# Expert results written to a row per token and choice instead of added to a row per token

## The chip, the cores and the metric

The kernel runs on one core of a Trainium2 chip. The metric is device time in microseconds (us). Engines: PE (TensorE, matrix products), DVE (VectorE), ACT (ScalarE), Pool (GpSimd), and SP, which here does nothing but issue transfers. Sixteen DMA engines carry out the transfers of all queues; SP's queue is q1 in the profile, Pool's queue q0. All data are float32; T = 1024 tokens, D = 1024 features.

## What is computed

Two transformer blocks one after the other: attention, a gated convolution FFN and a per-layer gate; then retention and a gated delta rule, and a mixture of 32 experts, closed by a norm. The change is in the mixture and the norm behind it:

```python
flat_e = (g_idx * EXPERTS_PER_GROUP + e_local).reshape(-1)   # two experts per token
order = jnp.argsort(flat_e)
tok = order // TOP_K
xs = xf[tok]
hid = silu(ragged_dot(xs, w1, group_sizes)) * ragged_dot(xs, w3, group_sizes)
ys = ragged_dot(hid, w2, group_sizes) * gate.reshape(-1)[order][:, None]
ffn = segment_sum(ys, tok, num_segments=n)
...
x = x + gate2[:, None, :] * ffn
return rmsnorm(x, final_norm_w)
```

So each token gets the sum of three rows: its own x (called x4 below) and the results of its two experts.

## The kernel before

The first block fills the span up to about 1430 us, the second block's mixers go to about 2260, then come the second half of the output projection with the router (2260 to 2360), the routing tables (2362 to 2385), the experts (2392 to 3025) and the final norm (3021 to 3061).

**Places.** The experts stand at 32 places of fixed size. The first three take 128 rows each; the others are ordered by their number of tokens, and the size of a place falls from 256 rows (two tiles) to 32 by a fixed list of steps. Places of up to 64 rows from the 16th on are "small". What doesn't fit is left to a loop (`left_over`, L1625 and after), which runs zero times for these inputs. All 36 tiles together have 3008 rows; the routing needs 2048. The order of work mixes large and small places and is written out by hand.

**Tables.** One-hot products give, for each row of each tile, its token plus one (0 where the row is empty). From this DVE makes two index tables: `tokI` for gathers, where an empty row names token 0, and `tabI` for scatters, where an empty row names a row of its own behind the tokens. `eidI` is the table of experts by place that SP reads to address weights. An empty row has gate 0.

**A place.** `gather` (L1467) is an indirect DMA on Pool: rows of h2 in DRAM into `xg`. PE transposes them, ACT and DVE split them in two parts (`xTh`, `xTl`). The twelve 512 KB blocks of an expert's weights come by `fetch` (L1238) on SP into a ring of 28 buffers (`r`, `Bh`, `Bl`, `x`), in order: each waits for its buffer to be free and for the transfer eight before it. Each block is split into `hi` (ACT, or Pool for some blocks, L80 and L86) and `lo` (DVE, L91). Products give `h`, `hid` (DVE, L1522 and L1542) and `y`. ACT copies y (L1580), Pool multiplies by the row `g2_row` (L1581) and issues the scatter (L1582), an indirect DMA that adds the tile's rows to rows of `y_d` in DRAM. `y_d` has T + 128 rows; x4 has been written to its first T rows, and the 128 behind them, cleared from a zeroed tile, take the empty rows. The two last places (30 and 31) scatter nothing: `keep` (L1585) holds their rows in `both`, in two parts.

**Final norm.** Eight fetches bring `y_d` back as tiles R[0] to R[7] (they wait for the last scatter), then the norm's weight row `fn`. `add_rows(t)` multiplies the one-hots of the last places' tokens by `both` on PE (L1683), adds the result to R[t] on DVE (L1684) and squares on ACT (L1685). `scales` (L1689 and the lines of `rsqrt`) makes the scale of four tiles in small DVE operations, `finish` scales a tile by it and by `fn`: odd tiles on ACT and Pool (L1694, L1695), even ones on DVE (L1697). Then the tile goes out (L1698). The order is four additions, scales, four additions, four finishes, scales, four finishes; the scheduler interleaves it on each engine.

**At the start of the FFN** (about 709 us) Pool only clears two columns of a buffer `gpad` (L614) now and then, SP loads weights and the convolution's taps `cw` (L580), and the additions of the convolution (L621) run on DVE.

Of the kernel before, what the change touches and what calls it, by code (L numbers as in the profile page):

```python
# [11 lines left out]
F32 = mybir.dt.float32  # L12
# [9 lines left out]
T = 1024  # L22
D = 1024
# [7 lines left out]
# steps of the delta rule after each product of the token-major projections, and how many of these come before them  # L31
LEAD, PACE = 3, (3,)
# blocks of an expert whose high parts are Pool's
HI_POOL = (2, 5, 8, 11)
# experts fetched before the counts are known; places with two tiles
NS, TWO = 3, 4
# buffers of weights (0 to 7: room of R; 8 to 23: room of B; others: their own) in the order of their use, and how many are filled after each tile
BUFS = [24, 25, 26] + [0, 1, 2, 8, 9, 10, 3, 11, 12, 13, 4, 14, 15, 5] + list(range(16, 24)) + [6, 7, 27, 28]
AHEAD = [1, 2, 2, 4, 4, 3, 1, 0]
# kinds of the places in their order: s fetched early, T two tiles, M up to 128 rows, L up to 64 rows  # L40
ORDER_OF = "sss" + "LLT" * 4 + "MMM" + "ML" * 6 + "LL"
# last steps: add rows, scales, finish a tile; tiles finished on Pool
GROUP = 3
# chunks of the retention that come before the output projection
RET, OUT_LAG, R_LAG = 2, 3, 2
FIN, FIN_POOL = "aaaacaaaaffffcffff", (1, 3, 5, 7)
# rows of a place: (from this place on, how many more)
STEPS = ((0, 128), (NS, 128), (NS + 1, -32), (NS + 2, -32), (NS + TWO, -64), (10, -32), (16, -32), (22, -16), (28, -16))
# first of the small places
# [3 lines left out]
def constants():  # L53
    """Tables that depend on shapes alone, one float32 array of 128 rows."""
# [28 lines left out]
def split(nc, src, hi, lo, hi_engine="act", lo_engine=None):  # L83
    """src = hi + lo exactly; both parts fit the float32r format."""
# [9 lines left out]
def rsqrt(nc, pool, x, y, n, tag="rsq"):  # L94
    """y = x ** -0.5 for small [128, n] tiles (first guess from the bits, then Newton)."""
# [10 lines left out]
def mm3(nc, ps, ah, al, bh, bl, start, stop, **kw):  # L106
    """ps += (ah + al)^T (bh + bl) without the product of the two low parts."""
    nc.tensor.matmul(ps, ah, bh, start=start, stop=False, **kw)  # L108
    nc.tensor.matmul(ps, ah, bl, start=False, stop=False, **kw)  # L109
    nc.tensor.matmul(ps, al, bh, start=False, stop=stop, **kw)  # L110


class Halves:
    """[128, NK, T] kept as two tiles, one for each half of T"""
# [11 lines left out]
def tile_kernel(ctx: ExitStack, tc: tile.TileContext, a: dict, out: bass.AP):  # L126
# [18 lines left out]
    def turn(out_, in_):  # L145
        """out_ <- in_^T"""
# [8 lines left out]
    # ------------------------------------------------------------------ x^T  # L155
# [6 lines left out]
    with ph:  # L162
# [45 lines left out]
        def forget_gates():  # L208
            """c = cumsum(log_sigmoid(f)), kept as -c in two parts"""
# [35 lines left out]
        def project(hp, begin=False):  # L245
            """k, q, v of two heads, feature-major; v is then turned to keys on partitions."""
# [123 lines left out]
        def attend(hp):  # L370
            """Scores of a block of queries go ahead of the products with v of the block before it."""
# [21 lines left out]
        # the first product starts on half of the tokens  # L393
# [13 lines left out]
        # ---- o^T of the other pairs, and p @ ple_w_proj (kept in DRAM), under the last pair  # L407
# [28 lines left out]
    # ------------------------------------------------------- shared from here on  # L436
    TW = dict(reuse_waits="tile")

    def row(pool_, src, name, bufs=None):
        """One row of DRAM on all partitions."""  # L440
# [4 lines left out]
    def layer_norm(pl, rs, g, b):  # L445
        """r <- LN(r) * g + b for a few tiles of tokens."""
# [15 lines left out]
    def rms_scale(pl, rs, y, junk):  # L462
        """y[:, i] <- (mean(rs[i]^2) + 1e-6)^-0.5"""
# [7 lines left out]
    def turn_in(psp, r, t, tag="pt"):  # L471
        """Bh/Bl[:, :, tile t] <- r^T in two parts."""
# [10 lines left out]
    def parts(src, pool_=None):  # L483
        """One [128, 1024] block of weights as two parts."""
# [6 lines left out]
    def load_res(w, more):  # L491
        """[1024, 1024] weights, one pair of parts for each row block."""
        return [parts(w[k * 128:(k + 1) * 128, :], pool_=None if k < 5 else more) for k in range(NK)]

    def token_mm(psp, t, w):
        """tile t of (B^T)^T @ w, 1024 columns in two banks."""
# [10 lines left out]
    # ------------------------------------------- output projection, residual, LN  # L507
# [22 lines left out]
    # ------------------------------------- modulation rows: silu(c) @ w_ada + b_ada  # L530
# [31 lines left out]
    # ------------------------------------------------------------- gated conv FFN  # L562
# [13 lines left out]
    with tc.tile_pool(name="ffn", bufs=2, **TW) as fp:  # L576
        w_up = a["ffn_w_up"][0]
# [10 lines left out]
        def need(key, ahead):  # L588
            """Weights in the order of their use, some ahead of it."""
# [1149 lines left out]
```

## Time and profile before

| | us |
|---|---|
| median of the runs | 3064.95 |
| lowest to highest of the three runs | 3062.79 to 3067.33 |
| span of the profiled execution | 3061.3 |
| PE busy in it | 2866.5 (94%) |
| DVE, ACT, Pool busy | 1765.7, 1016.4, 644.7 |
| moved by DMA | 432.4 MB, 141 GB/s over the span |

The median lies 3.65 us above the profiled span. A window's row gives, for each engine, busy time and the number of instructions, then the clock granted to PE (1.00 is the full 2.4 GHz), the mean busy share of the DMA engines (it can come out a little over 1) and what they moved. In a timeline a row is one instruction or a run of alike ones: start, duration, engine, line, operation, what it writes and reads, and in brackets how long the engine stood idle before it and what ended that.

### The profile page before, as it was taken

What the parts mean: (1) busy time and instruction counts of PE and PEld (TensorE: products, weight loads), DVE (VectorE), ACT (ScalarE), POOL (GpSimd) and SP (SyncE); (2) the same over time, 40 slices, a digit from 0 to 9 for tenths busy, and PEclk for the clock granted to TensorE, in tenths of its full rate; (3) what the DMA queues carried; (4) which work ended last, traced back from release to release, by engine and by line L of the source; (5) the groups of instructions that cost most, each with busy time, mean ns of one, the idle gap of its engine ahead of it and who ended that gap; (6) DMA issues with size and microseconds to landing.
All of it is one profiled execution on the core that took longest, in us unless ns stands there. A gap on an engine that the chain in (4) does not pass through costs nothing. (4 is left out here: it accounts for less than half of the span.)

```text
span 3061.3 us, 38090 instructions
## 1 busy us (share of the span) xinstructions
PE 2866.5 (94%) x13899; PEld 2168.0 (71%) x13899; DVE 1765.7 (58%) x3066; ACT 1016.4 (33%) x1773; POOL 644.7 (21%) x622
## 2 busy tenths in 40 slices
PE   7999999899999999999989999999996799998985
PEld 5777777677787877877767888888775655465441
DVE  4666666556555454555956545544578743358654
ACT  3555555612121221221324321222222433244432
POOL 2333332100000000000120023211222434444542
PEclk9999999999999999999998999999998899999997
DMA  3110111424233232232244412222557799998997
GB/s 99 36 32 29 35 32 41 163 79 111 69 97 97 69 110 72 73 110 83 97 80 89 92 66 66 80 76 76 195 166 248 252 339 334 329 322 290 362 374 279
DMA packets 272681, 432.39 MB, mean 141 GB/s; under 512 B 40550, under 2 KB 135910, under 8 KB 272364
## 3 DMA queue, kind: packets, MB, share of 16 engines
q1 hardware_dynamic: 264908, 405.41, 40.3%
q0 software_dynamic: 7584, 24.52, 3.4%
q8 instruction: 111, 1.82, 0.2%
q14 instruction: 78, 0.64, 0.1%
HBM read 373.61 MB, written 56.25 MB: 140 GB/s over the span
## 5 line engine op out<-in xcount | busy, mean ns | idle before, releaser
L108 PE MATMUL g<-Bh,hi 128*128 128x512 f32 x896 | 357.9, 400 | 5.1 <-ACT hi L86 3.9
L109 PE MATMUL g<-Bl,hi 128*128 128x512 f32 x896 | 356.7, 398 | 3.3 <-DVE Bl L91 3.3
L110 PE MATMUL g<-Bh,lo 128*128 128x512 f32 x896 | 356.9, 398 | 1.1 <-DVE lo L91 1.1
L108 PE MATMUL g<-hi,Bh 128*128 128x512 f32 x704 | 282.8, 406 | 4.9 <-ACT hi L86 4.0
L109 PE MATMUL g<-lo,Bh 128*128 128x512 f32 x704 | 281.7, 402 | 0.7 <-DVE lo L91 0.7
L110 PE MATMUL g<-hi,Bl 128*128 128x512 f32 x704 | 282.2, 402 | 0.0
L86 ACT ACTIVATE hi<-wst 128x1024 fp32r<-128x1024 f32 x122 | 128.3, 1058 | 430.9 <-PE g L110 207.8
L91 DVE TENSOR_TENSOR lo<-wst,hi 128x1024 fp32r<-128x1024 f32 x122 | 149.0, 1226 | 187.4 <-ACT hi L86 186.6
L108 PEld LDWEIGHTS g<-Bh,hi 128*128 128x128 f32 x896 | 169.1, 189 | 47.2 <-ACT hi L86 4.6
L109 PEld LDWEIGHTS g<-Bl,hi 128*128 128x128 f32 x896 | 169.4, 189 | 45.1 <-DVE Bl L91 4.1
L110 PEld LDWEIGHTS g<-Bh,lo 128*128 128x128 f32 x896 | 169.5, 189 | 42.8 <-DVE lo L91 1.9
L614 POOL MEMSET gpad<- 128x2 f32 x22 | 2.2, 100 | 787.6 <-DVE cacc L621 658.2
L108 PE MATMUL g<-Bh,wh 128*128 128x512 f32 x384 | 155.3, 404 | 5.4 <-DVE k L262 3.6
L108 PEld LDWEIGHTS g<-hi,Bh 128*128 128x128 f32 x704 | 133.2, 189 | 33.8 <-ACT hi L86 5.2
L109 PE MATMUL g<-Bl,wh 128*128 128x512 f32 x384 | 155.9, 406 | 0.0
L110 PE MATMUL g<-Bh,wl 128*128 128x512 f32 x384 | 155.3, 404 | 0.0
L109 PEld LDWEIGHTS g<-lo,Bh 128*128 128x128 f32 x704 | 133.6, 190 | 29.3 <-DVE lo L91 1.8
L110 PEld LDWEIGHTS g<-hi,Bl 128*128 128x128 f32 x704 | 133.3, 189 | 29.4 <-DVE Bl L91 0.9
L109 PE MATMUL h<-lo,xTh 128*128 128x512 f32 (+2 forms) x320 | 130.2, 407 | 16.0 <-DVE lo L91 16.0
L331 POOL TENSOR_SCALAR P<-P,l 128x384 f32<-128x384 f32 (+7 forms) x128 | 96.6, 759 | 224.3 <-DVE l L330 162.0
L109 PE MATMUL g<-lo,hh 128*128 128x512 f32 x352 | 140.3, 399 | 0.0
L108 PE MATMUL g<-hi,hh 128*128 128x512 f32 x352 | 139.9, 397 | 0.0
(525 smaller groups left out, 6333.6 us busy)
## 6 DMA issues: line engine op xcount, KB each, us to landing
r<-in_w_dram SPq DMA_DIRECT2D x107, 512.0 KB, 10.7
Bh<-in_w_dram SPq DMA_DIRECT2D x105, 512.0 KB, 10.5
Bl<-in_w_dram SPq DMA_DIRECT2D x104, 512.0 KB, 10.7
x<-in_w_dram SPq DMA_DIRECT2D x68, 512.0 KB, 10.5
wst<-in_w_ada_dram SPq DMA_DIRECT2D x48, 512.0 KB, 3.9
wst<-in_ffn_w_up_dram SPq DMA_DIRECT2D x44, 512.0 KB, 3.7
wst<-in_w_in_dram SPq DMA_DIRECT2D x32, 512.0 KB, 6.0
wst<-in_attn_w_in_dram SPq DMA_DIRECT2D x24, 512.0 KB, 3.8
```

Of the source, the lines that this page charges most:

```text
L86: nc.scalar.activation(hi, src, AF.Copy)
L91: (lo_engine or nc.vector).tensor_tensor(lo, src, hi, op=OP.subtract)
L108: nc.tensor.matmul(ps, ah, bh, start=start, stop=False, **kw)
L109: nc.tensor.matmul(ps, ah, bl, start=False, stop=False, **kw)
L110: nc.tensor.matmul(ps, al, bh, start=False, stop=stop, **kw)
L331: nc.gpsimd.tensor_scalar(p[:, :n], p[:, :n], l[:, 0:1], 1.0, op0=OP.mult, op1=OP.mult)
L614: nc.gpsimd.memset(gp[f][:, 0:2], 0.0)
```

## The change

`y_d` gets 2 T rows, one for each token and choice (row token + choice x T). It is allocated at the start of the FFN and cleared there by two DMAs on Pool, in 4096 pieces of 1 KB each, out of one 128x256 tile of zeros. The scatter writes instead of adding; so no row is written twice. An empty row gets an index past the end in both tables, and gather and scatter pass over indices past a bound (T - 1 for gathers, 2 T - 1 for scatters). Since a gather now leaves the empty rows of `xg` as they were, both `xg` buffers (and the two of the loop for left-over tiles) are cleared once on Pool before the first gathers. x4 goes to a DRAM tensor of its own. In the final norm SP fetches eight tiles of x4 and then sixteen tiles of `y_d`; for each tile of tokens Pool adds the first choice's rows, and PE adds the second choice's by a product with the identity into the bank that already takes the last places' rows.

```diff
+        y_d = dram.tile([2 * T, D], F32, name="y_d")
+        zero = fp.tile([128, 256], F32, name="zero", bufs=1)
+        nc.gpsimd.memset(zero, 0.0)
+        for k in range(2):
+            nc.gpsimd.dma_start(y_d[k * T:(k + 1) * T, :].rearrange("(p t) (c f) -> p (t c) f", p=128, f=256),
+                                zero[:, None, :].to_broadcast([128, 32, 256]))
...
-    y_d = dram.tile([T + 128, D], F32, name="y_d")
+    x4_d = dram.tile([T, D], F32, name="x4_d")
...
-            nc.sync.dma_start(y_d[t * 128:(t + 1) * 128, :], R[t])
+            nc.sync.dma_start(x4_d[t * 128:(t + 1) * 128, :], R[t])
...
-        V.tensor_tensor(val, oht[k], ids[:, :, None].to_broadcast([128, NT, NTAB]), op=OP.mult)
+        V.scalar_tensor_tensor(val, ids[:, :, None].to_broadcast([128, NT, NTAB]), float(k * T), oht[k],
+                               op0=OP.add, op1=OP.mult)
...
-    V.tensor_scalar(tokI, pt_, -1.0, 0.0, op0=OP.add, op1=OP.max)
+    emp, tg = tl([128, NTAB], "emp"), tl([128, NTAB], "tg")
+    V.tensor_scalar(emp, pt_, 0.0, 4.0 * T, op0=OP.is_equal, op1=OP.mult)
+    V.scalar_tensor_tensor(tabI, pt_, -1.0, emp, op0=OP.add, op1=OP.add)
+    V.tensor_scalar(tg, pt_, float(T + 1), -float(T), op0=OP.is_ge, op1=OP.mult)
+    V.tensor_tensor(tokI, tabI, tg, op=OP.add)
     V.scalar_tensor_tensor(eidI, tokI[0:1, 0:NE], 0.0, pe, op0=OP.mult, op1=OP.add)
-    emp, tg = tl([128, NTAB], "emp"), tl([128, NTAB], "tg")
-    posr = tl([128, 1], "posr")
-    V.tensor_scalar(posr, col_i, float(T + 1), None, op0=OP.add)
-    V.tensor_scalar(emp, pt_, 0.0, posr, op0=OP.is_equal, op1=OP.mult)
-    V.tensor_tensor(tg, pt_, emp, op=OP.add)
-    V.tensor_scalar(tabI, tg, -1.0, None, op0=OP.add)
...
         nc.gpsimd.indirect_dma_start(out=xg[0:n, :], out_offset=None, in_=h2_d[:, :],
-                                     in_offset=bass.IndirectOffsetOnAxis(ap=idx, axis=0))
+                                     in_offset=bass.IndirectOffsetOnAxis(ap=idx, axis=0),
+                                     bounds_check=T - 1, oob_is_err=False)
...
             nc.gpsimd.indirect_dma_start(out=y_d[:, :], out_offset=bass.IndirectOffsetOnAxis(ap=dst, axis=0),
-                                         in_=ys[0:n_, :], in_offset=None, compute_op=OP.add)
+                                         in_=ys[0:n_, :], in_offset=None, bounds_check=2 * T - 1, oob_is_err=False)
...
-    zero = wst.tile([128, D], F32, name="wst")
-    nc.gpsimd.memset(zero, 0.0)
-    nc.sync.dma_start(y_d[T:T + 128, :], zero)
+    for _ in range(2):
+        nc.gpsimd.memset(mo.tile([128, D], F32, name="xg", bufs=2), 0.0)
+        nc.gpsimd.memset(wst.tile([128, D], F32, name="wst"), 0.0)
...
-    R = [fetch(y_d[t * 128:(t + 1) * 128, :]) for t in range(NT)]
+    R = [fetch(x4_d[t * 128:(t + 1) * 128, :]) for t in range(NT)]
+    Y = [[fetch(y_d[k * T + t * 128:k * T + (t + 1) * 128, :]) for k in range(2)] for t in range(NT)]
...
     def add_rows(t):
+        nc.gpsimd.tensor_tensor(R[t], R[t], Y[t][0], op=OP.add)
         for c in range(2):
             cs = slice(c * 512, (c + 1) * 512)
             ps = ps_h.tile([128, 512], F32, name="h")
-            mm(ps, oh[:, t * 128:(t + 1) * 128], both[:, cs], start=True, stop=True)
+            mm(ps, ident, Y[t][1][:, cs], start=True, stop=False)
+            mm(ps, oh[:, t * 128:(t + 1) * 128], both[:, cs], start=False, stop=True)
             nc.vector.tensor_tensor(R[t][:, cs], R[t][:, cs], ps, op=OP.add)
```

In the changed kernel the lines stand 7 to 11 higher (L1582 is L1589, L1684 is L1695).

**SP at the end of the program**, from the last block of weights on (`Bh<-in_w_2_dram` is that block; `y_d` is the table of results, `x_d` in the second piece the tensor x4). Before:

```order
L1238 DMA Bh_18416<-in_w_2_dram 128x1024
L1238 DMA Bh_18416<-y_d 128x1024 x2
L1238 DMA r_23922<-y_d 128x1024
L1238 DMA Bh_18416<-y_d 128x1024
L1238 DMA Bl_18417<-y_d 128x1024 x2
L1238 DMA r_23927<-y_d 128x1024
L1238 DMA Bl_18417<-y_d 128x1024
L442 DMA xTh<-in_final_norm_w_dram 128x1024
```

After, up to the first four blocks of the second choice's buffers:

```order
L1245 DMA Bh_18421<-in_w_2_dram 128x1024
L1245 DMA Bh_18421<-x_d 128x1024 x2
L1245 DMA r_24074<-x_d 128x1024
L1245 DMA Bh_18421<-x_d 128x1024
L1245 DMA Bl_18422<-x_d 128x1024 x2
L1245 DMA r_24079<-x_d 128x1024
L1245 DMA Bl_18422<-x_d 128x1024
L1245 DMA Bl_18422<-y_d 128x1024
L1245 DMA r_24083<-y_d 128x1024
L1245 DMA Bh_18780<-y_d 128x1024 x4
L1245 DMA Bl_18781<-y_d 128x1024 x4
```

Eight fetches became twenty-four (six more `y_d` fetches follow), and the norm's row still comes behind all of them; the wait for the last scatter moved from the first of the eight to the first `y_d` fetch.

**Pool before the first gathers** (`gval` are values for the gate table, `xg` the gathered rows, `ovI` the number of left-over tiles that the loop reads). Before:

```order
L91 TENSOR_TENSOR lo<-r_18375,hi 128x1024
L1440 TENSOR_TENSOR gval_18998<-oht_18935,gh 128x8x58
L1440 TENSOR_TENSOR gval_18998<-oht_18935,gl 128x8x58
L1440 TENSOR_TENSOR gval_19009<-oht_18949,gh 128x8x58
L1440 TENSOR_TENSOR gval_19009<-oht_18949,gl 128x8x58
L1467 DMA xg<-h_d,tokI 128x1024 x2
L1628 TENSOR_LOAD ovI
```

After:

```order
L1446 TENSOR_TENSOR gval_19001<-oht_18940,gh 128x8x58
L1446 TENSOR_TENSOR gval_19001<-oht_18940,gl 128x8x58
L1446 TENSOR_TENSOR gval_19012<-oht_18954,gh 128x8x58
L1446 TENSOR_TENSOR gval_19012<-oht_18954,gl 128x8x58
L1603 MEMSET xg 128x1024 x2
L1473 DMA xg<-h_d,tokI 128x1024 x2
L1636 TENSOR_LOAD ovI
```

Two clearings of `xg` came between the last of the `gval` operations and the gathers.

**DVE in the final norm**, from the additions of tile 5 on (`Bh`, `Bl`, `r` are tiles of R, `h` the bank with the rows to add, `fin_t`, `fin_u`, `ss`, `rms_y` the small operands of the scales). After:

```order
L1695 TENSOR_TENSOR Bl_18422<-Bl_18422,h 128x512 x2
L1695 TENSOR_TENSOR r_24079<-r_24079,h 128x512 x2
L1695 TENSOR_TENSOR Bl_18422<-Bl_18422,h 128x512
L1708 SCALAR_TENSOR_TENSOR Bh_18421<-Bh_18421,rms_y_24116,xTh 128x1024
L1695 TENSOR_TENSOR Bl_18422<-Bl_18422,h 128x512
L1708 SCALAR_TENSOR_TENSOR r_24074<-r_24074,rms_y_24116,xTh 128x1024
L1700 TENSOR_SCALAR ss_24117<-ss_24117 128x4
```

Before, the last additions stood among the small operations of the first four tiles' scales, and both finishing operations behind all of them:

```order
L1684 TENSOR_TENSOR Bl_18417<-Bl_18417,h 128x512
L103 SCALAR_TENSOR_TENSOR rms_y_23941<-fin_t,rms_y_23941 128x4
L1684 TENSOR_TENSOR Bl_18417<-Bl_18417,h 128x512
L101 TENSOR_TENSOR fin_t<-rms_y_23941 128x4
L102 SCALAR_TENSOR_TENSOR fin_t<-ss_23942,fin_t 128x4
L103 SCALAR_TENSOR_TENSOR rms_y_23941<-fin_t,rms_y_23941 128x4
```

The scales of the first four tiles moved ahead of the last three tiles' additions, and tile 0's finishing operation ahead of the very last addition.

At the start of the FFN Pool's row of work was 22 clearings of `gpad`; it is now one clearing of `zero`, two of `gpad`, the two DMAs `y_d<-zero`, and the other twenty of `gpad`.

## Rows read from the trace of the kernel before

**Rows 1.** The page: one engine's busy time, share and instructions; one queue's packets, MB, share.

```profile
PE 2866.5 (94%) x13899; PEld 2168.0 (71%) x13899; DVE 1765.7 (58%) x3066; ACT 1016.4 (33%) x1773; POOL 644.7 (21%) x622
...
q0 software_dynamic: 7584, 24.52, 3.4%
```

**Rows 2.** Windows: from:to, length, busy us (instructions) by engine, PE clock, DMA share, GB/s.

```profile
700.00:750.00 50.00, 48.93 (x218) 39.14 (x217) 34.10 (x52) 15.14 (x20) 0.30 (x3) 1.00 0.54 132
720.00:730.00 10.00, 9.43 (x45) 7.49 (x44) 5.69 (x8) 3.98 (x7) 0.00 (x0) 1.00 0.87 87
2380.00:3020.00 640.00, 588.62 (x2652) 339.80 (x2654) 340.10 (x302) 233.57 (x341) 274.85 (x169) 0.97 0.96 328
2480.00:2720.00 240.00, 231.43 (x1063) 132.65 (x1060) 88.42 (x86) 74.70 (x118) 95.45 (x57) 0.99 1.00 348
2860.00:3011.00 151.00, 140.44 (x648) 67.17 (x648) 73.37 (x62) 52.12 (x83) 63.87 (x41) 0.99 1.04 370
```

**Rows 3.** Waits of SP's queue, 2480 to 2720: who waits <- for whom, us, times, longest.

```profile
SPq L1238 <- PE h L1517: 53.1, 20, 10.6
```

**Rows 4.** Waits of SP's queue, 2860 to 3011.

```profile
SPq L1238 <- DMA Bl<-in_w_dram: 22.9, 26, 2.3
SPq L1238 <- DMA Bh<-in_w_dram: 18.6, 22, 2.5
SPq L1238 <- DMA r<-in_w_dram: 17.0, 24, 1.3
SPq L1238 <- DMA x<-in_w_dram: 14.2, 14, 2.1
```

**Rows 5.** Timeline of SP at the end (duration is of the issues).

```profile
3009.13 0.33 SPq L1238 DMA_DIRECT2D Bh<-in_w_dram  x1
3010.90 1.66 SPq L1238 DMA_DIRECT2D Bh<-y_d  x2
...
3020.06 0.32 SPq L1238 DMA_DIRECT2D Bl<-y_d  x1
3021.34 0.34 SPq L442 DMA_DIRECT2D xTh<-in_final_norm_w_dram  x1
```

**Rows 6.** DMA queues, 2860 to 3011: packets, MB, share of 16 engines.

```profile
q1 hardware_dynamic: 22396, 51.08, 90.7%
q0 software_dynamic: 1440, 4.72, 13.5%
```

**Rows 7.** Pool's queue from 2384 to 2394; then 3004.4 to 3020, with issue to landing.

```profile
q0 software_dynamic: 288, 1.05, 31.8%
...
q0 software_dynamic: 48, 0.13, 4.3%
...
y_d<-wst,tabI POOLq DMA_INDIRECT x1, 6.1
```

**Rows 8.** Waits of PE, 2380 to 3040.

```profile
PE h L109 <- DVE lo L91: 16.0, 17, 2.1
...
PE t L148 <- SPq L1619: 7.5, 1, 7.5
```

**Rows 9.** Timeline of DVE and Pool around 2530.

```profile
2529.91 4.52 DVE L91 TENSOR_TENSOR lo<-Bl,hi 128x1024 fp32r<-128x1024 f32 x2
...
2530.86 2.48 POOL L1581 TENSOR_TENSOR wst<-wst,g_row 128x1024 f32<-128x1024 f32 x1
```

**Rows 10.** Timeline of Pool: FFN start, first gathers, last scatter.

```profile
748.75 0.10 POOL L614 MEMSET gpad<- 128x2 f32 x1 [38.89 <-DVE cacc L621]
...
2383.46 1.08 POOL L1467 DMA_INDIRECT xg<-h_d,tokI  x1 [0.84 <-DVE eidI L1407]
2384.85 0.97 POOL L1467 DMA_INDIRECT xg<-h_d,tokI  x1 [0.30 <-POOLq L1629]
...
3004.36 1.35 POOL L1582 DMA_INDIRECT y_d<-wst,tabI  x1 [0.28 <-POOL wst L1581]
```

**Rows 11.** Timeline of DVE in the final norm: first and last addition, a scale operation.

```profile
3025.67 2.48 DVE L1684 TENSOR_TENSOR Bh<-Bh,h 128x512 f32<-128x512 f32 x4
...
3035.24 0.68 DVE L1684 TENSOR_TENSOR Bl<-Bl,h 128x512 f32<-128x512 f32 x1
...
3039.42 2.31 DVE L1689 TENSOR_SCALAR ss<-ss 128x4 f32<-128x4 f32 x1
```

**Rows 12.** Waits of DVE, 705 to 750.

```profile
DVE cacc L621 <- DMA cw<-in_ffn_conv_w_dram: 0.9, 1, 0.9
```

More of the change, by code (lines that the diff above doesn't have):

```diff
@@ L1673, in tile_kernel @@
         assert n == 32
-        nc.vector.tensor_copy(tok_c[32 * i:32 * i + 32, :], tabI[0:32, c_:c_ + 1])
+        nc.vector.tensor_copy(tok_c[32 * i:32 * i + 32, :], tokI[0:32, c_:c_ + 1])
     oh = mo.tile([128, T], F32R, name="xTl", bufs=2)
```

## The prediction

> **What bounds the kernel now.** I read the page first, then the experts' stretch in windows, then who waits for whom in it, then the last 60 us row by row. TensorE is busy 94% of the span, and the Pool engine's DMA queue takes only 3.4% of the DMA engines' time [rows 1], so an average over the span says that indirect transfers are nearly free. The windows say otherwise for one stage: from 2480 on the DMA share is 1.00, and 1.04 from 2860 to 3011, while PE is busy 231.4 of 240 us and 140.4 of 151 us [rows 2]. Both are close to full there. Which one leads is seen at SP, which issues the experts' weights in order into 28 buffers. From 2480 to 2720 its longest wait is for TensorE to free a buffer (53.1 us) [rows 3]: TensorE leads, and less DMA traffic buys nothing. From 2860 to 3011 its four longest waits are for earlier weight transfers, 22.9 + 18.6 + 17.0 + 14.2 = 72.7 us [rows 4]: DMA leads. TensorE does not feel this, since SP runs some 28 blocks ahead of it; what is set there is the time at which the last weight is issued, 3009.13, and with it the final fetches from 3010.90 to 3020.06 [rows 5]. So the case is decided in the last 150 us.
>
> **The price of a row.** In 2860 to 3011 Pool's queue moved 1440 packets in 13.5% of 151 us, 20.4 us of all sixteen engines; the weights took 90.7% [rows 6]. Of these 1152 are rows of 4 KB, half gathered and half accumulated, and the others are small closing packets. A stretch with the first two gathers alone: 31.8% of 10 us on 16 engines for 256 rows, 0.199 us for a gathered row. A stretch with the last scatter alone: 4.3% of 15.6 us for 32 rows, 0.335 us for an accumulated row [rows 7]. Check: 576 x (0.199 + 0.335) / 16 = 19.2 us of the 20.4.
>
> **Experts: fewer and cheaper rows.** The places hold 3008 rows, and the routing that follows from the reference's own inputs fills 2048. Gathers fall from 3008 to 2048 rows, scatters from 2944 to 2028 (the last two places stay on chip). Of the 1152 rows after 2860 629 remain. A plainly written row stands nowhere in the trace; I bound it by a gathered row (0.199) and an accumulated one (0.335). 629 rows then take 7.8 to 10.5 us instead of 19.2 to 20.4: 9 to 12.6 us less, in the very stretch where SP waits for DMA. I take 10.5 (a write without a read is nearer to a gather). If skipped rows still cost a packet, the saving is 576 x 0.136 / 16 = 4.9 us at most.
>
> The same saving before 2860 (by the same prices 20 to 38 us of DMA time) lies beside a TensorE that leads, and I cost it at nothing. What could come of it is TensorE waiting less: it waits 16.0 us for `lo` [rows 8]. `lo` is late where DVE and Pool work on the same moments: a `lo` pair took 4.52 us while Pool multiplied for 2.48 us [rows 9], and such Pool multiplications stay. Pool's own time in a scatter (1.35 us for 32 rows [rows 10]) should hardly change. I take -3 us here, between 0 and -12: a fifth of the waits for `lo`.
>
> **Last stage: 16 fetches more.** Before, eight 512 KB fetches go out between 3010.90 and 3020.06, 1.31 us apart, then the weight row of the norm at 3021.34 [rows 5]. The additions on DVE follow from 3025.67 and end at 3035.24 + 0.68 = 3035.9 [rows 11]; 25.4 us later the span ends (3061.3). Now x4's eight tiles go first, then sixteen tiles of y, then the norm's row: 16 x 1.31 = 20.9 us of transfers more. Two things soften it. First, x4 no longer waits for the scatters; only the first y fetch does. The last scatter is issued at 3004.36 [rows 10] and lands 6.1 us later [rows 7], about when the fetches began before. So if the weights end early enough, x4 goes under the experts. Eight fetches take 10.4 us, so the last weight has to leave by about 2999, 9.9 us earlier than now. The 10.5 us just taken would pay for that, and no more can be won, since y's first fetch waits for the last scatter. Second, DMA now sets the pace of the additions, so the scales of the first four tiles (and tile 0's last step) run while y arrives.
>
> With all of it: y from 3010.9 to 3030.5, the norm's row 3031.8, landing some 10 us later at about 3042. In DVE's order tile 0's last step, which needs that row, stands ahead of the very last addition: 3042 + 1.3 + 0.7 = 3044.0. From there 25.4 us as before, less some 2.3 us already done: 3067.1, that is +5.8. With no relief (last weight at 3009.1): y from 3020.9 to 3040.5, all 10 us later: 3077, +15.8.
>
> Who works on it: Pool adds one of the two y rows (128x1024, 2.4 us as in its multiplications [rows 9]), one in 2.6 us, so it keeps up. TensorE adds the other through an identity product, sixteen products into an otherwise idle engine: nothing. DVE's additions have one operand in PSUM; I take them as unhurt by Pool. The small scale operations are hurt: one took 2.31 us beside Pool [rows 11], and some now stand beside Pool's additions. This is in the 10 us of slack that y's pace gives: nothing, at most +4.
>
> **Start of the experts.** The first gathers left at 2383.46 and 2384.85 [rows 10], and the experts' first products waited 7.5 us for the loop behind them [rows 8]. Now two clearings of `xg` stand ahead of them on Pool, the second waiting for the products that end about 2384.8; about 1 us each, so the gathers leave some 2.5 us later. `tokI`, until now the first of the small DVE operations on the table, becomes the fourth; that hides under the clearing. With 83 and 66 rows in place of 128 each they land sooner by up to a microsecond. +1.7, between 0 and +3.
>
> **Zero fill of y.** 8.4 MB in 8192 pieces of 1 KB on Pool's queue when the FFN begins. Pool's next work there is the third `gpad` at 748.75, which Pool waited 38.89 us for [rows 10], and the DMA share from 700 to 750 is 0.54 (0.87 from 720 to 730, when the taps of the convolution are loaded) [rows 2]. A piece costs between a quarter of a gathered row (0.05 us) and a whole one: 25 to 102 us of all engines, beside a TensorE that is busy 48.9 of 50 us [rows 2]. DVE waited 0.9 us for the taps [rows 12]; some microseconds more there would reach TensorE only past its store of work. I take 0, between 0 and +10. It would cost much if Pool stayed in these two instructions beyond 38.9 us. 32 rows hold Pool 1.35 us, 128 rows 0.97 in a gather, so nearly all of it is fixed, and I take it as covered.
>
> What speaks against this point stands in the Trainium skill, "DMA: Bandwidth & Descriptors", section "SWDGE vs HWDGE vs iDMA": Pool writes the descriptors of its DMAs into SBUF, in the same state that DVE locks it out of in its two-port mode. The trace shows DVE and Pool holding each other up in tensor operations [rows 9], not a large issue by Pool beside DVE. By the rule the two instructions might outlast their 38.9 us of cover; by the row on issue cost they don't.
>
> **The sum.** +5.8 (last stage) + 1.7 (start) - 3 (experts) + 0 (FFN) = +4.5. Span 3061.3 + 4.5 = 3065.8; the median lies 3.65 above the profiled span, so 3069.5. A change under 0.2%, 6.1 us, can hardly be told from none here.
>
> **Rivals.** (A) Slower: the relief does not bring the last weight forward. The waits of [rows 4] may be no queueing for bandwidth but the pace of eight transfers in flight, or the buffers are freed no earlier. Then the tail's 20.9 us come after the experts: 15.8 + 1.7 - 3 = +14.5, 3079.5. It decides from a last weight later than about 3002. For it: y's fetches have nothing to hide under. Against: the DMA share of 1.04. (B) Faster: the traffic and accumulation removed all through the experts, 31 to 48 us of DMA time by the prices above, shorten TensorE's own waits (16.0 us for `lo` and others [rows 8]; 640 - 588.6 = 51 us idle from 2380 to 3020 [rows 2]). If a third of it goes: 4.5 - 15 = -10.5, 3054.5. Against: it waits for other engines, not for DMA. (C) The passed-over rows still cost packets: 4.9 us of relief, so 10.9 + 1.7 - 3 = +9.6, 3074.5. (D) Slower: Pool's descriptors for the zero fill outlast the cover. If a sixth of the 1.35 us for 32 rows grew with their number, 4096 pieces would take 29 us and both instructions 58, 19 beyond the cover: +19 on top of the forecast, 3088.5.
>
> **How the numbers follow.** The forecast has 0.48 (+4.5, from some -2 to +10; 0.39 of it within 0.2% and 0.09 above), A 0.15, B 0.24, C 0.07, D 0.06. Faster is B, 0.24; same 0.39; slower is the forecast's upper part, A, C and D: 0.37. The range goes from B's time to just past A's, 3054 to 3083, and leaves out D and the far half of B.
>
> **What would show it.** The last weight issued near 2999 and the first y fetch near 3011 (forecast); near 3009 and 3021 (A). Pool's queue after 2860 with about 629 rows and a share near 6%; with 1152 rows (C). Pool's third `gpad` near 748.8 (else D). TensorE's idle time from 2392 to 3020 down by more than 10 us would be B. Scatters that take longer to land than accumulating ones would make all of it wrong.

## The result: 0.6% slower

The changed kernel takes 3083.49 us (median of four runs, 3082.34 to 3087.11) beside 3066.14 us of the kernel before on the same chip: a ratio of 1.0061, with a 95% interval of 1.0047 to 1.0075. The prediction was 3069.5 us, range 3054 to 3083, "no change" as the likeliest. The time lies just past the upper end, and the direction is the one that the forecast gave 0.37. The profiled execution has a span of 3082.2 us, 20.9 more than the one before.

Where the 20.9 us come in is read by the start of the same operation in both traces:

| operation | before | after | shift so far |
|---|---|---|---|
| first operation of the FFN's convolution (DVE) | 724.93 | 743.93 | +19.0 |
| table of experts, `eidI` (DVE) | 2383.27 | 2404.00 | +20.7 |
| last scatter (Pool) | 3004.36 | 3014.78 | +10.4 |
| end of the span | 3061.3 | 3082.2 | +20.9 |

So three things happened: 19 us lost in front of the convolution, some 10 us won in the experts, 10.5 us lost in the last stage. Of the 1.7 us between the convolution and `eidI`, 0.6 go to the table operations that now stand ahead of it; the rest I can't put to a cause. Windows of the changed kernel, with the columns of [rows 2]:

```profile
700.00:750.00 50.00, 33.26 (x139) 26.54 (x138) 21.29 (x36) 7.00 (x10) 3.92 (x5) 0.83 0.78 225
...
720.00:730.00 10.00, 2.89 (x13) 2.01 (x12) 0.76 (x2) 0.00 (x0) 0.00 (x0) 0.88 1.03 364
730.00:740.00 10.00, 1.30 (x5) 1.16 (x6) 2.42 (x3) 2.66 (x5) 0.00 (x0) 0.50 1.03 363
...
2870.00:3021.00 151.00, 142.09 (x654) 68.38 (x654) 73.62 (x64) 53.14 (x84) 60.40 (x42) 0.98 1.03 379
```

TensorE, busy 9.43 of 10 us from 720 to 730 in [rows 2], is busy 2.89 and then 1.30 of 10 us, and its granted clock fell to 0.50 on the way, while the DMA engines are full (1.03). The waits of TensorE and of DVE from 705 to 760 name what is late:

```profile
PE pt L148 <- DVE Bl L91: 15.8, 1, 15.8
```

```profile
DVE lo L91 <- ACT hi L86: 16.7, 3, 16.1
```

And the tile of weights behind that `lo` says what ACT waited for: the fourth block of `ffn_w_up`, issued on SP at 715.8.

```profile
  DMA wst<-in_ffn_w_up_dram: 21.3, 1
```

How the wait passes from engine to engine, before and after (`pt` is the bank into which TensorE transposes the last tiles of tokens, `Bl` what DVE makes of it):

```profile
720.45 1.23 DVE L91 TENSOR_TENSOR lo<-wst,hi 128x1024 fp32r<-128x1024 f32 x1 [0.83 <-ACT hi L86]
721.59 1.28 DVE L91 TENSOR_TENSOR Bl<-pt,Bh 128x512 fp32r<-128x512 f32 x2
...
736.82 1.22 DVE L91 TENSOR_TENSOR lo<-wst,hi 128x1024 fp32r<-128x1024 f32 x1 [16.06 <-ACT hi L86]
737.97 1.28 DVE L91 TENSOR_TENSOR Bl<-pt,Bh 128x512 fp32r<-128x512 f32 x2
...
738.70 1.11 PE L148 MATMUL pt<-ident,r 128*128 128x128 f32 x4 [15.81 <-DVE Bl L91]
```

TensorE did not yet need the late block: it was at the end of the second block's products (44 on record since 710.5, 24 to a block). It needed the bank `pt`, and the `Bl` that frees it stands behind the late block's `lo` in DVE's order.

The queues from 705 to 750 and Pool's timeline show what was in front of it:

```profile
q0 software_dynamic: 2080, 8.39, 53.8%
q1 hardware_dynamic: 13882, 2.84, 33.0%
```

```profile
710.82 3.46 POOL L582 DMA_DIRECT2D y_d<-zero  x2 [0.24 <-POOL gpad L621]
```

The two clearing DMAs went out at 710.82 and held the DMA engines for 53.8% of 45 us, 24.2 us. The block of weights was issued 5 us later. The two queues from 725 to 728, on its way:

```profile
q0 software_dynamic: 259, 1.00, 89.5%
q1 hardware_dynamic: 258, 0.13, 14.5%
```

So the block did not wait for the end of the zeros, which still moved 127 packets from 740 to 743. The packets of the two queues went one for one, from 722 to 734 almost to the packet, and a packet of the block has 512 bytes where one of the zeros has 4 KB. From 716 to 719 no packet of the block came; in the kernel before, 997 packets of SP's queue went in these 3 us. The taps waited as well:

```profile
721.03 23.80 SPq L587 DMA_DIRECT2D cw<-in_ffn_conv_w_dram  x3
```

The last stage, on SP and DVE (before: [rows 5] and [rows 11]):

```profile
3011.87 0.33 SPq L1245 DMA_DIRECT2D Bh<-in_w_dram  x1
3013.17 1.67 SPq L1245 DMA_DIRECT2D Bh<-x_d  x2
...
3023.90 0.32 SPq L1245 DMA_DIRECT2D Bl<-y_d  x1
...
3039.21 4.86 SPq L1245 DMA_DIRECT2D x<-y_d  x4
3044.97 0.34 SPq L442 DMA_DIRECT2D xTh<-in_final_norm_w_dram  x1
```

```profile
3049.00 1.03 DVE L1700 TENSOR_SCALAR ss<-ss 128x4 f32<-128x4 f32 x1 [1.35 <-ACT xg L1696]
...
3050.75 1.80 DVE L99 TENSOR_SCALAR rms_y<-fin_u 128x4 int32<-128x4 int32 x1
...
3052.79 2.32 DVE L102 SCALAR_TENSOR_TENSOR fin_t<-ss,fin_t 128x4 f32<-128x4 f32 x1
...
3061.60 0.68 DVE L1695 TENSOR_TENSOR Bl<-Bl,h 128x512 f32<-128x512 f32 x1
```

Pool's additions beside them:

```profile
3047.64 2.37 POOL L1689 TENSOR_TENSOR Bl<-Bl,r 128x1024 f32<-128x1024 f32 x1 [0.18 <-issue]
3050.18 2.35 POOL L1689 TENSOR_TENSOR r<-r,x 128x1024 f32<-128x1024 f32 x1 [0.17 <-DMA x<-y_d]
3052.75 2.34 POOL L1689 TENSOR_TENSOR Bl<-Bl,x 128x1024 f32<-128x1024 f32 x1 [0.22 <-DMA x<-y_d]
```

Three of the scales' small operations, 0.16 us each by themselves, took 1.03, 1.80 and 2.32 us, each until one of these additions ended (3050.01, 3052.53 and 3055.09); DVE's additions of tiles 5 to 7 stand behind them.

### The profile page after: what moved, and what is told of

The parts are those of the page before. It is cut to its first block, busy times and chain, and to the rows that moved or that the text cites. A ratio compares the mean times of both kernels' runs of the same rounds, so it can differ in the third digit from the quotient of the medians.

```text
span 3082.2 us, 38291 instructions
## 1 busy us (share of the span) xinstructions
PE 2876.8 (93%) x13931; PEld 2175.1 (71%) x13931; DVE 1763.1 (57%) x3065; ACT 1015.0 (33%) x1773; POOL 652.7 (21%) x636
```

## Experiments: where the 19 us come from

Two theories stood for the FFN. Burst: the zeros come among loads that the engines need within a few microseconds. Rival: the changed order of instructions there, or Pool's own time, costs it.

**The clearing alone**, added to the kernel before (of a DRAM tensor that nothing reads):

```diff
+        f_d = dram.tile([2 * T, D], F32, name="f_d")
+        zf = fp.tile([128, 256], F32, name="zf", bufs=1)
+        nc.gpsimd.memset(zf, 0.0)
+        for k in range(2):
+            nc.gpsimd.dma_start(f_d[k * T:(k + 1) * T, :].rearrange("(p t) (c f) -> p (t c) f", p=128, f=256), ...)
```

> The kernel before, with nothing but the clearing of 8.4 MB at the FFN's start added (of a DRAM tensor that nothing reads). Theory (burst): +19 us, about 3084 to 3085, with TensorE idle from 720 to 740. Rival (the rest of the change at the FFN's start costs it): within 3 us of the kernel before.

Measured: 3083.82 us, ratio 1.0058 (1.0038 to 1.0078). The convolution's first operation starts at 741.73, and TensorE shows the same hole:

```profile
720.00:730.00 10.00, 0.36 (x2) 0.00 (x0) 0.00 (x0) 0.00 (x0) 0.00 (x0) 0.73 1.04 362
730.00:740.00 10.00, 3.70 (x13) 3.23 (x14) 3.75 (x5) 3.71 (x6) 0.00 (x0) 0.50 1.01 339
```

The clearing suffices; nothing else of the change is needed for the loss.

**The clearing in eight pieces, meant for the attention:**

```diff
+        def fill(c):
+            nc.gpsimd.dma_start(y_d[256 * c:256 * c + 256, :]..., zero[:, None, :].to_broadcast([128, 8, 256]))
...
+            for c in {0: (), 1: (0, 1)}.get(hp, (hp,)):
+                fill(c)
             w = load_w_cols(2 * D + hp * 128)
```

> The changed kernel, but the 8.4 MB of zeros go out in eight pieces of 1 MB during the attention, one or two for each pair of heads, where the DMA engines are busy a tenth of the time. Theory (the burst of zeros delays the weights and taps that the FFN needs within the next 10 us, and TensorE runs dry for 19 us): the first convolution starts near 725 as before, and the whole is about 19 us faster than the changed kernel, 3064 to 3066 us. Rival (the changed order of DVE's and SP's instructions at the FFN's start, or DMA issue on Pool itself, costs the time): no more than 5 us faster, about 3080.

Measured: 3084.37 us, 1.0064 (1.0047 to 1.0081), no better than the change, which looks like the rival. The timeline of Pool shows that the experiment was not the one meant:

```profile
3.20 5.53 POOL L184 DMA_DIRECT2D y_d<-zero  x6
42.28 1.76 POOL L184 DMA_DIRECT2D y_d<-zero  x2
```

The pieces wait for nothing but a tile of zeros, so the scheduler put six of them at the very start, among the loads of the first tiles of x and the first weights. Windows of TensorE there (before it is busy 6.46 and 10.00 us):

```profile
10.00:20.00 10.00, 2.95 (x13) 2.34 (x13) 2.71 (x4) 1.79 (x3) 0.00 (x0) 1.00 1.01 362
20.00:30.00 10.00, 1.06 (x5) 0.66 (x4) 1.38 (x2) 1.62 (x3) 0.00 (x0) 1.00 0.92 323
```

The attention's last scores end 17 us late (591.14 against 574.19), and up to the FFN's last operation of the convolution the delay grows only to 18.4 us. The burst was paid at another place.

**The same bytes, paced.** Each piece's zeros are made from a product of a hidden tile, so that it can't leave early:

```diff
+            if hf == 0 and 2 <= f < 18:
+                zero = fp.tile([128, 256], F32, name="zero", bufs=1)
+                nc.gpsimd.tensor_scalar(zero, acc[:, 0:256], 0.0, None, op0=OP.mult)
+                c0 = 128 * (f - 2)
+                nc.gpsimd.dma_start(y_d[c0:c0 + 128, :].rearrange("p (c f) -> p c f", f=256), ...)
```

> The changed kernel, with the same 8.4 MB of zeros in sixteen pieces of 512 KB, one with each of the FFN's hidden tiles 2 to 17; the tile of zeros is made from a product of that hidden tile, so that a piece can't leave before it. Theory (it was the burst in front of urgent loads, not the bytes): 3063 to 3067 us, no stall of TensorE at 720 to 740, and as fast as with the small zero scatters. Rival (8.4 MB more on the DMA engines cost their time anywhere): 3075 to 3084 us.

Measured: 3068.17 us, 1.0004 (0.9993 to 1.0014), 1 us above the theory's range but far from the rival's. From the convolution's first operation (726.38) to its last in the FFN (1436.40) it takes 710.0 us, as before (724.93 to 1434.97). The 8.4 MB cost nothing measurable when their pieces come one by one.

**No large clearing at all.** Every row of the table is written by a scatter, but for those of the two places kept on chip. Two small scatters of zero rows write these:

```diff
+    z_ = wst.tile([128, D], F32, name="wst")
+    nc.gpsimd.memset(z_, 0.0)
+    for p_ in places[NE - 2:NE]:
+        (n_z, c_z), = where(p_)
+        nc.gpsimd.indirect_dma_start(out=y_d[:, :], out_offset=...(ap=tabI[0:n_z, c_z:c_z + 1], axis=0),
+                                     in_=z_[0:n_z, :], in_offset=None, bounds_check=2 * T - 1, oob_is_err=False)
```

> The changed kernel without the clearing of 8.4 MB. What needs zeros are only the rows that no scatter writes, those of the two places kept on chip; two small scatters of zero rows (32 rows each, empty ones passed over) write them before the experts begin. Theory (a burst of zeros costs 17 to 19 us wherever the DMA engines or TensorE need loads soon after; the rest of the change is +10.5 us in the last stage against -10.8 us in the experts): 3063 to 3067 us, the convolution's first operation near 725 and the last scatter near 2994. Rival (the loss sits in the program's other changes and moves with them, as it stayed when the zeros were moved): 3080 or more.

Measured: 3064.01 us, 1.0000 (0.9987 to 1.0012); the last scatter at 2991.87. The theory held: without the burst the rest of the change comes out even.

## Experiments: what shortened the experts

From the third gather to the last scatter the kernel before takes 609.7 us (2394.70 to 3004.36), the changed one 598.9 (2415.89 to 3014.78). I had predicted 3 us. Two theories: S, the 960 gathered and 916 scattered rows that are passed over; W, that rows are written and not added.

**Passing over alone**, with adding and the short last stage (both `xg` buffers are cleared as in the change):

```diff
-    V.tensor_scalar(tokI, pt_, -1.0, 0.0, op0=OP.add, op1=OP.max)
+    V.tensor_scalar(emp, pt_, 0.0, 4.0 * T, op0=OP.is_equal, op1=OP.mult)
+    V.scalar_tensor_tensor(tokI, pt_, -1.0, emp, op0=OP.add, op1=OP.add)
...
-                                         in_=ys[0:n_, :], in_offset=None, compute_op=OP.add)
+                                         in_=ys[0:n_, :], in_offset=None, compute_op=OP.add,
+                                         bounds_check=T - 1, oob_is_err=False)
```

> The kernel before, with only the passing over of empty rows: gathers and scatters skip indices past T - 1, the scatters still add into the one row of a token, the last stage fetches eight tiles as before, and there is no clearing of a large table. Theory S (the experts' stretch got 10.8 us shorter since 960 gathers and 916 scattered rows are gone): about -9 us, 3055 to 3058 us, Pool's queue with some 4800 packets fewer bytes by a third. Rival W (it got shorter since a row is written and not read, added and written): within 3 us of the kernel before, 3063 to 3067 us.

Measured: 3068.17 us, 1.0013 (1.0001 to 1.0025): no gain, if anything a loss; the same stretch takes 614.9 us.

**Writing without passing over** (empty rows gather token 0 and go to 128 rows behind the table; zeros as in the eight pieces, so its 17 us are in the total):

```diff
-                                     bounds_check=T - 1, oob_is_err=False)
...
-                                         in_=ys[0:n_, :], in_offset=None, bounds_check=2 * T - 1, oob_is_err=False)
+                                         in_=ys[0:n_, :], in_offset=None)
```

> As the run with the zeros in the attention, but no row is passed over: empty rows gather token 0 and are written to 128 rows of their own behind the table. Theory S (skipping shortened the experts): the experts' stretch takes some 8 to 11 us longer than with skipping, the whole 3073 to 3076 us. Rival W (writing shortened them): within 3 us of the run with skipping.

Measured: 3085.09 us, 1.0062 (1.0042 to 1.0082); the stretch takes 598.9 us (2414.27 to 3013.15), as with passing over. W holds, S falls. The two runs tell more. Pool's queue from 2400 to 3011 and the scatters on Pool, first of the run that passes over and adds:

```profile
q0 software_dynamic: 6592, 15.94, 11.3%
```

```profile
L1580 POOL DMA_INDIRECT y_d<-wst,tabI x34 | 69.1, 2033 | 9.9 <-POOL wst L1579 3.1 <-issue 2.1 <-POOL hi L80 2.0
```

and of the run that writes all rows:

```profile
q0 software_dynamic: 7024, 24.25, 11.3%
```

```profile
L1595 POOL DMA_INDIRECT y_d<-wst,tabI x34 | 50.2, 1476 | 8.2 <-POOL wst L1594 2.8 <-issue 2.1 <-POOL hi L80 2.1
```

Both relieve the DMA engines alike, to 11.3% of the stretch (16.1% before). One of them gains 11 us and the other nothing. What differs is how long a scatter holds Pool: 2033 ns when adding, 1476 ns when writing. A scatter that adds also lands later (median 7.9 us after its issue, against 6.8), but in the stretch only one operation waited for such a landing, for 1.9 us.

**Writing alone**, with nothing else of the change:

```diff
-                                         in_=ys[0:n_, :], in_offset=None, compute_op=OP.add)
+                                         in_=ys[0:n_, :], in_offset=None)
```

> The kernel before, with the scatters writing instead of adding and nothing else changed: the last stage still fetches eight tiles, so the sum over a token's rows is left out. Theory W (writing alone, through Pool's half microsecond less in each scatter, shortens the experts by 10 to 11 us): 3052 to 3055 us, Pool's mean scatter 1.48 instead of 2.04 us, the last scatter near 2994. Rival (the gain needs the whole change, as the earlier x4 fetches or the fewer rows): within 3 us of the kernel before.

Measured: 3052.72 us, 0.9957 (0.9941 to 0.9974). That is the price of adding, 13 us, seen by itself. It stands in every trace: from the third gather to the last scatter TensorE is idle for 41.2 to 41.7 us in the four kernels that add (606.7 to 614.9 us long), and for 33.2 to 35.2 us in the nine that write and leave Pool alone (595.9 to 599.8).

**Writing alone, and Pool kept busy:**

```diff
+            nc.gpsimd.tensor_scalar(ys[0:n_, 0:512], ys[0:n_, 0:512], 1.0, None, op0=OP.mult)
             nc.gpsimd.indirect_dma_start(out=y_d[:, :], ...)
```

> The kernel before with scatters that write instead of adding (so the sum over a token's rows is left out, as in the run of the writing alone), and Pool multiplies half of each result tile by one ahead of the scatter, about 0.5 us of Pool's time each, 34 times. Theory (writing gains through Pool's time: 0.56 us less in each scatter, so that DVE and the blocks that Pool splits are less late): most of the 13 us are lost again, 3061 to 3066 us. Rival (writing gains since the DMA engines don't read what they add to): 3052 to 3056 us as with writing alone.

Measured: 3078.44 us, 1.0039 (1.0026 to 1.0053), 26 us more than writing alone. The dose was larger than meant:

```profile
L1582 POOL TENSOR_SCALAR wst<-wst 128x512 f32<-128x512 f32 (+4 forms) x34 | 61.3, 1802 | 1.3
```

61.3 us of Pool's time cost 23 us in the stretch (598.3 to 621.6 us), 0.38 us per microsecond; the 19.1 us that writing saves (69.3 of the kernel before against 50.2) gave 11.4 us, 0.60 per microsecond. So Pool's time does bear on the experts' pace, in about the size needed, though Pool is busy less than half of the stretch. How it gets to DVE, in DVE's wait for the blocks that Pool splits, before, with writing alone and with Pool kept busy (from the third gather to the last scatter):

```profile
DVE lo L91 <- POOL hi L80: 126.4, 36, 11.7
DVE lo L91 <- POOL hi L80: 113.2, 33, 12.3
DVE lo L91 <- POOL hi L80: 142.9, 45, 12.5
```

And from DVE to TensorE, waits of TensorE from 2393 to 3025 in the run with writing alone:

```profile
PE h L109 <- DVE lo L91: 13.2, 12, 2.1
PE t L148 <- DVE hid L1522: 8.1, 5, 2.4
PE t L148 <- DVE hid L1542: 6.5, 7, 1.4
```

Before it is 16.0 [rows 8], 10.0 and 8.9: 7.1 us less wait for DVE. With Pool kept busy the three are 13.4, 9.6 and 14.9. The rest of the 11.4 us is no wait. The three stretches as windows, in the same order:

```profile
2394.70:3004.36 609.66, 567.98 (x2556) 329.25 (x2557) 332.11 (x281) 228.46 (x333) 269.10 (x165) 0.98 0.97 332
2393.42:2991.71 598.29, 563.77 (x2556) 328.93 (x2557) 326.57 (x281) 228.44 (x333) 249.16 (x164) 0.98 0.95 342
2398.26:3019.82 621.56, 575.19 (x2564) 332.33 (x2565) 324.51 (x281) 229.38 (x334) 305.89 (x198) 0.96 0.93 332
```

With writing alone TensorE is idle for 34.5 us instead of 41.7, 7.2 us less, and the same 2556 products take 4.2 us less: in slices of 20 us its granted clock is below 1.00 in six of 30, before in ten of 31. With Pool kept busy 11.9 of the 23 us are idle time and 11.4 products, at a mean clock of 0.96; so the two rates per microsecond are rough.

The added operation might have slowed DVE itself, since tensor operations of Pool and DVE hold each other up [rows 9]. It did not: DVE's 281 instructions take 324.5 us with it and 326.6 without. That the microseconds saved in a scatter act like those added here, through the blocks that Pool splits, fits all of these waits, but no run changes only the time of a scatter's issue.

## Experiments: the last stage

The run with the small zero scatters has the long last stage, the run of writing alone the short one. From the last scatter to the end they take 67.8 us (2991.87 to 3059.7) and 57.2 us (2991.71 to 3048.9): 10.6 us is the price of the longer last stage, its sixteen fetches and Pool's additions together.

**Norm's row first, tiles 6 and 7 on TensorE** (on top of the small zero scatters; run twice):

```diff
+    fn = row(mo, a["final_norm_w_2"][None, :], "xTh", 2)
     Y = [[fetch(...) for k in range(2)] for t in range(NT)]
-    fn = row(mo, a["final_norm_w_2"][None, :], "xTh", 2)
...
-        nc.gpsimd.tensor_tensor(R[t], R[t], Y[t][0], op=OP.add)
+        by_pe = Y[t] if t > 5 else Y[t][1:]
+        if t <= 5:
+            nc.gpsimd.tensor_tensor(R[t], R[t], Y[t][0], op=OP.add)
```

> As the run with the small zero scatters, and in the last stage the norm's row is fetched ahead of the sixteen tiles of y, and for tiles 6 and 7 both rows are added by products on TensorE, so that Pool is idle when DVE works on the scales. Theory (in the last stage DVE's small operations wait for Pool's additions, 5 to 6 us, and the last addition waits for the norm's row): 4 to 6 us faster than the run with the small zero scatters, 3058 to 3062 us, faster than the kernel before. Rival (the sixteen fetches alone set the end): within 1.5 us of it.

> The run with the changed last stage (norm's row first, tiles 6 and 7 added on TensorE, tiles 5 and 7 finished on ACT and Pool) once more, since its profile began the experts some 7 us late for no reason in the change. Theory: 3058 to 3062 us beside a kernel before of about 3065. Rival: 3064 to 3067 us again.

Measured: 3065.59 us, 0.9991 (0.9980 to 1.0002), and 3061.63 us, 0.9991 (0.9981 to 1.0001). In the traces the last stage is 64.7 and 64.3 us from the last scatter to the end, 3 us less than with all of Pool's additions (67.8); the small operations of the scales run at 0.16 us, but for one of 0.96 us in the second trace. As a whole neither run can be told from the one without it (1.0000), and the first lies outside the range of its theory.

**Tiles 5 and 7 finished on DVE as well:**

```diff
-FIN, FIN_POOL = "aaaacaaaaffffcffff", (1, 3, 5, 7)
+FIN, FIN_POOL = "aaaacaaaaffffcffff", (1, 3)
```

> As the run with the changed last stage (norm's row first, tiles 6 and 7 added on TensorE), and tiles 5 and 7 are finished on DVE instead of ACT and Pool. Theory (the last four finishes wait on DVE and Pool holding each other up): some 2 us faster than that run, 3058 to 3063 us, and faster than the kernel before by 3 us or more. Rival: the last stage is set by the fetches and the transfer out; no difference from that run, nor from the kernel before.

Measured: 3056.96 us, 0.9966 (0.9954 to 0.9978), faster than both kernels. The last finishes follow one another on DVE:

```profile
3046.28 2.48 DVE L1712 SCALAR_TENSOR_TENSOR Bl<-Bl,rms_y,xTh 128x1024 f32<-128x1024 f32 x2
3048.68 1.28 DVE L1712 SCALAR_TENSOR_TENSOR r<-r,rms_y,xTh 128x1024 f32<-128x1024 f32 x1
3049.87 1.28 DVE L1712 SCALAR_TENSOR_TENSOR Bl<-Bl,rms_y,xTh 128x1024 f32<-128x1024 f32 x1
```

where the changed kernel had

```profile
3067.27 1.28 DVE L1708 SCALAR_TENSOR_TENSOR Bl<-Bl,rms_y,xTh 128x1024 f32<-128x1024 f32 x1
3068.47 3.45 DVE L1708 SCALAR_TENSOR_TENSOR r<-r,rms_y,xTh 128x1024 f32<-128x1024 f32 x1
```

with Pool at tiles 5 and 7 until 3074.1. From the last scatter to the end it is 58.9 us (2996.53 to 3055.4), only 2 us above the short stage of the kernel before (56.9), with the sixteen fetches.

**The same two tiles in the kernel before:**

> The kernel before, with only tiles 5 and 7 finished on DVE instead of ACT and Pool. Theory (the last four finishes wait on DVE and Pool holding each other up, in the kernel before as well): 2 to 4 us faster, 3061 to 3064 us, and that part of the fastest version's gain has nothing to do with writing. Rival (the finishes matter only behind the longer last stage): no difference.

Measured: 3062.61 us, 0.9992 (0.9983 to 1.0002). Its profiled run has 51.2 us from the last scatter to the end (56.9 before), but the times together give 2.5 us, and the interval holds no change. So part of what the fastest version gains, some 3 to 6 us, belongs to these two tiles and not to writing, and beside a last stage of 51.2 us the longer one still costs 7.7 (58.9).

The theory explains only a third of the 5.7 us in the trace. The last transfer out, before and here:

```profile
3052.91 0.33 SPq L1698 DMA_DIRECT2D out_dram<-Bl  x1
...
3046.39 0.33 SPq L1698 DMA_DIRECT2D out_dram<-Bl  x1
```

It is issued 48.6 and 46.6 us after the last scatter, 2.0 us apart, and from there to the end it is 8.4 and 4.6 us. The traces don't say why. The pair with the longer stage shows the same: 1.5 us up to that issue and 3.9 behind it.

## Why the prediction was wrong

**Zero fill: the step that failed.** I put 25 to 102 us of all DMA engines on it, and the lower end was right: 24.2 us. (The 8192 pieces of 1 KB went as 2080 packets, so mostly four pieces to a packet, 0.186 us each.) The step that failed is the cover. I named "a TensorE that is busy 48.9 of 50 us" as the work that hides it, said that a delay at the taps would reach TensorE "only past its store of work", and took 0, between 0 and +10, without asking how large that store is and what else is loaded there. It lasted from the issue of the next block of weights at 715.8 until 722.7, 7 us, while the block reached ACT 20 us after its issue. And it ran out early, since ACT and DVE work in order: the last transposed tiles stood behind the late block. Of the loads I had only looked at the taps; the same block is issued at 714.62 in the kernel before and split on ACT from 719.35.

A better sum counts packets. The block's 512 KB are 1024 packets of 512 bytes; if each lets one of the zeros' packets pass, that is 1024 x 0.186 / 16 = 11.9 us, and 3 us in which none came: an estimate of 15 us. Measured: DVE's wait of 16.1 us, where it was 0.8. The rest of the 19.0 us: DVE was 1.2 us later already before this wait, waited 1.0 us longer for the transposes behind it, which ran at a granted clock of 0.50 (1.2 GHz) after TensorE's idle time, and 1.5 us for the taps.

For rival D I looked at Pool's issue time instead. That was no trouble: 3.46 us for both instructions, so that D's price of +19 is the measured one by luck. The rule from the Trainium skill ("DMA: Bandwidth & Descriptors", "SWDGE vs HWDGE vs iDMA") that DVE in its two-port mode keeps Pool from writing descriptors had no effect here: both were out within 3.5 us beside a DVE that was busy 8.62 of 10 us from 710 to 720. In which mode DVE's operations ran no row shows, so the rule itself is not tested.

**Experts: the right sign, the wrong cause.** I predicted -3 us and got -10.8. "Pool's own time in a scatter should hardly change" was wrong: it fell from 2039 to 1485 ns, and by the runs above the gain goes with it; the DMA time, on which I had built, gave nothing before the last weights (TensorE idle for 41.6 us with passing over alone, 41.7 before). I had one row of 1.35 us for a scatter and no written one, and bounded only the DMA price of a row, not the price on Pool. Rival B named the place, TensorE's waits, but too large a size (a third of its 51 us, 17; the idle time fell by 8.4) and the wrong reason.

**Relief before the last weights: held, a little short.** The last weight leaves 2.9 us before the last scatter is issued, where it left 4.8 after it: 7.7 us of the 9.9 needed. (With passing over alone it leaves 2.1 us before, with writing alone 2.0; so either of the two gives most of it.) The first y fetch goes 9.1 us after the last scatter instead of the 6.5 assumed: 2.6 us lost. Pool's queue takes 5.0% from 2870 to 3021, where I expected 6, and 13.5% in [rows 6]. Rivals A and C fall. Yet the packets of the passed-over rows are still there: 1440, as in [rows 6], with 2.58 MB in place of 4.72. They cost next to nothing: 5.0% of 151 us on 16 engines is 0.192 us for each of 629 rows.

**Last stage: +5.8 predicted, +10.5 measured.** The fetches took 21.1 us from the first y to the norm's row (20.9 predicted). The last addition came 5.3 us later than they explain; 4.7 of that are the scales' three operations that waited for Pool's additions. I had seen this effect and priced it at nothing, at most +4, with the y pace as cover; the additions stand behind those operations on DVE, so there was no cover. In return the end is 19.9 us after the last addition where I had 23.1. 2.6 + 5.3 - 3.2 = 4.7.

**Start of the experts:** +1.7 predicted; from `eidI` to TensorE's first work on gathered rows it is 9.64 us (2404.00 to 2413.64) against 9.19 before, +0.5. The fewer rows did not land sooner (5.8 us against 5.9). What I had too dear was the clearing: the first gather leaves 0.84 us after `eidI`, 0.19 before.

**The sum.** 19.0 + 1.7 + 0.5 - 10.8 + 10.5 = 20.9. Without the burst the change comes out even (1.0000), near the +4.5 of the forecast, but by luck: the experts gave 7.8 us more than I had and the last stage took 4.7 more.

## What to carry to other kernels

A busy engine hides a burst of transfers only for as long as its own work lasts without the loads that are issued behind the burst. So look at what is issued in the microseconds after it, at how large the packets of those loads are, and at what stands behind their consumers in the order of the other engines. A clearing that waits for nothing can be moved ahead by the scheduler, as in the run with eight pieces, among the first loads of the program. Tie it to work, in small pieces, or clear only the rows that nobody writes: both cost nothing measurable here. An indirect transfer has a price on the engine that issues it (here 1.5 to 2.0 us) beside its price on the DMA engines, and where DVE waits for Pool that one can decide.

## What the runs showed of the hardware that I had not expected

A scatter that adds holds Pool some 0.55 us longer than one that writes (2039 against 1485 ns on average, 1.35 against 0.89 us for 32 rows), whether or not rows are passed over (2033 and 2039 with adding, 1485 and 1476 with writing). A written row is no dearer for the DMA engines than a gathered one (0.199 us): with all rows moved and none added, 11.3% of 611 us on 16 engines for 24.25 MB, or 5920 rows, is 0.187 us a row, gathered and written together, where an added one had 0.335 us. A passed-over row keeps its packet in the queue's count, but costs next to nothing. Two queues that both had work waiting sent their packets one for one, so a load in packets of 512 bytes went at the pace of a clearing in packets of 4 KB: 258 packets and 0.13 MB of the one beside 259 and 1.00 MB of the other in 3 us. And a DVE operation on 128x4 numbers took up to 2.32 us beside an addition on Pool, while DVE's additions with one operand in PSUM kept their 0.69 us, as I had assumed.
